# A batched matmul with scale and add on one core: one load per piece of x, another order of transfers, eight shared semaphores, and sixteen tiny loads

## The chip, the core and the metric

The kernel runs on one core of a Trainium2 chip. A core has five engines that run their own instruction lists beside each other: TensorE (PE, matmul), VectorE (DVE), ScalarE (ACT), GpSimd (POOL) and SyncE (SP), which here issues the DMA transfers. Sixteen DMA engines move the data between the chip's memory (HBM) and the core's own memory (SBUF); the matmul writes its sums to PSUM. Engines wait for each other by semaphores. The metric is the time of one execution on the device in microseconds (us). Before the change it is 209.91 us, the median of three runs that lie between 209.87 and 209.99.

## The reference

```python
batch, m, k, n = 16, 512, 1024, 768        # all float32; scale = 0.1
out = scale * np.matmul(x, weight) + add_value
```

x is 16 x 512 x 1024, weight 1024 x 768 and shared by the batch, add_value and the output 16 x 512 x 768. Flattened, it is one matmul of 8192 x 1024 by 1024 x 768 with an element-wise end. Reading x, add_value and weight and writing the output makes 87 MB.

## The kernel before

**Tiles.** The 8192 rows are 64 tiles of 128 rows (`T`). The row that partition p holds in tile t is chosen so that consecutive tiles of one partition lie next to each other in HBM: a transfer of 8 tiles is, for each of 128 partitions, one contiguous piece (32 KB of x, 24 KB of add_value or output). A tile of one tensor is called a slot here. In SBUF there are 16 slots for x (`xs`), used as a ring, and 32 slots for add_value (`ao`), also a ring; the result overwrites add_value in its slot, and the output is written from there. The weights arrive as float32 in slots 16 to 23 of `ao` before add_value needs these.

**The stream.** The string `STREAM` sets the order of all transfers: `x16+8` is x, tiles 16 to 23, `a` is add_value, `o` the output, `w` the weights. SyncE goes through it in order (`sync_engine`), on one queue. Before each transfer it waits for what that transfer needs: an x piece for the casts that empty its slots of the ring (`by_act`, `by_pool`), an add_value piece for the landing of the output that used its slots before (`carriers`), an output for the VectorE work on its tiles (`made`). A transfer behind a waiting one waits too. Each of the 27 transfers in the block has a semaphore of its own that tells of its landing (`landed`). The last one, `o60+4`, is issued behind the block, when all engines are through.

**Moves.** For four tiles at a time (`mover`, 16 moves) ScalarE and GpSimd cast x to bf16, eight casts each, on 32 partitions at a time and regrouped by quarters, into one of two buffers `va`. They start a move when its x has landed and the buffer is free.

**Turns.** VectorE transposes two tiles at a time in blocks of 32 x 32 (`turn`), on pairs of bf16 values taken as one float32, into one half of `xt`; with the regrouping in the moves this is the transpose of the whole 128 x 128 piece.

**Matmuls.** TensorE loops over groups of four tiles (`tensor_engine`). For each tile there are eight pieces of x of 128 x 128 (`KJ`), and each is multiplied with 768 columns of the weights in two matmuls, of 512 and of 256 columns (`CUT`), since a PSUM bank holds 512 float32 of a partition. `xt[q, j // 2]` is the stationary operand, loaded into the array by a weight load (PEld, LDWEIGHTS) that goes with every matmul.

**Finish.** VectorE multiplies the sums of two tiles by the scale and adds add_value, in one instruction (`finish`), and signals `made`. It then transposes the pair after next.

Of the kernel before, what the change touches and what calls it, by code (L numbers as in the profile page):

```python
# [7 lines left out]
P = 128  # L8
G = 16
X_SLOTS = 16  # L10
A_SLOTS = 32
W_SLOT = 16
CUT = 512
MM_BUFS = 4
XT_TILES = 4
VA_BUFS = 2
MOVE = 4

STREAM = """
    x0+4 w0+4 w4+4 x4+8 a0+8 a8+8 x12+4 x16+8 a16+16 x24+8 o0+8 x32+8 o8+8 a32+8 x40+8  # L20
    a40+8 x48+8 o16+8 o24+8 a48+4 x56+8 a52+4 a56+8 o32+16 o48+4 o52+8 o60+4
"""


def transfers():
    for word in STREAM.split():
        s, n = word[1:].split("+")
        yield word[0], int(s), int(n)
# [3 lines left out]
def kernel(  # L32
# [8 lines left out]
    nc = tc.nc  # L41
    bf16 = mybir.dt.bfloat16
    fp32 = mybir.dt.float32
# [5 lines left out]
    _, N = weight.shape  # L49
    T = M // P  # L50
    MOVES = T // MOVE
    KC = K // (2 * P)
    KJ = 2 * KC
# [6 lines left out]
    def rows(view, s, n):  # L60
        assert s // G == (s + n - 1) // G
        return view[:, s // G, s % G:s % G + n, :]

    const = ctx.enter_context(tc.tile_pool(name="const", bufs=1))
# [4 lines left out]
    w_bf = const.tile([P, KJ, N], bf16, name="w_bf")  # L69
    va = [const.tile([P, MOVE * KC, 4, 64], bf16, name=f"va{i}") for i in range(VA_BUFS)]  # L70
    xt = const.tile([P, XT_TILES, KC, P], fp32, name="xt")
    mm = psum.tile([P, MM_BUFS, 1024], fp32, name="mm")

    stream = list(transfers())
    landed = [tc.alloc_semaphore(f"{op}{s}") for op, s, n in stream[:-1]]
    by_act, by_pool, pool_go, turned, casts, done, made = (
        tc.alloc_semaphore(name)
        for name in ("by_act", "by_pool", "pool_go", "turned", "casts", "done", "made"))
    TURNED = MOVE * VA_BUFS
    MADE = TURNED + MM_BUFS  # L80

    def carriers(op, s, n):
        return [sem for (o, a, k), sem in zip(stream, landed)
                if o == op and a < s + n and s < a + k]

    def slots(op, s, n):
        ring = X_SLOTS if op == "x" else A_SLOTS
        k = s % ring
        assert k + n <= ring
        return slice(k, k + n)  # L90

    def engine(eng):
        known = {}

        def need(sem, value):
            if known.get(sem.num if hasattr(sem, "num") else id(sem), 0) < value:
                eng.wait_ge(sem, value)  # L97
                known[sem.num if hasattr(sem, "num") else id(sem)] = value

        return need  # L100

    def transfer(eng, op, s, n):
        if op == "w":
            dst = ao[:, W_SLOT + s:W_SLOT + s + n, :].rearrange("p (c r) n -> p c (r n)", r=2)
            return eng.dma_start(dst, w_v[:, s // 2:(s + n) // 2, :])  # L105
        if op == "x":
            return eng.dma_start(xs[:, slots(op, s, n), :], rows(x_v, s, n))  # L107
        if op == "a":
            return eng.dma_start(ao[:, slots(op, s, n), :], rows(add_v, s, n))  # L109
        return eng.dma_start(rows(out_v, s, n), ao[:, slots(op, s, n), :])  # L110

    def sync_engine(eng):
        need = engine(eng)
        for (op, s, n), sem in zip(stream, landed):
            last = s + n
            if op == "x" and last > X_SLOTS:
                moved = 8 * -(-(last - X_SLOTS) // MOVE)
                need(by_act, moved)
                need(by_pool, moved)
            if op == "a":  # L120
                if s < W_SLOT + KJ <= A_SLOTS and last > W_SLOT:
                    need(casts, KJ)
                if s >= A_SLOTS:
                    for old in carriers("o", s - A_SLOTS, n):
                        need(old, 16)
            if op == "o":
                need(made, MADE + last)
            transfer(eng, op, s, n).then_inc(sem, 16)

    def mover(eng, copy, parity, count, go=None):  # L130
        need = engine(eng)
        if go is None:
            eng.preload_act_table(mybir.ActivationFunctionType.Copy)  # L133
        for q in range(MOVES):
            for sem in carriers("x", MOVE * q, MOVE):
                need(sem, 16)
            if q >= VA_BUFS:
                need(turned, TURNED + MOVE * (q - VA_BUFS + 1))
            if go is not None:
                eng.sem_inc(go, 1)  # L140
            k = MOVE * q % X_SLOTS
            src = xs[:, k:k + MOVE, :].rearrange("p i (c b k) -> p (i c) b k", b=4, k=64)
            for a in (parity, parity + 2):
                for b in range(4):
                    copy(va[q % VA_BUFS][32 * b:32 * b + 32, :, a, :],  # L145
                         src[32 * a:32 * a + 32, :, b, :]).then_inc(count, 1)

    def vector_engine(eng):
        need = engine(eng)

        def cast_w(s, n):
            for sem in carriers("w", s, n):
                need(sem, 16)
            eng.tensor_copy(w_bf[:, s:s + n, :], ao[:, W_SLOT + s:W_SLOT + s + n, :]).then_inc(casts, n)  # L154

        def turn(pair):
            move, half = divmod(pair, 2)
            need(by_act, 8 * (move + 1))
            need(by_pool, 8 * (move + 1))
            if pair > 1:  # L160
                need(done, 4 * (pair - 1))
            q = 2 * half * KC
            eng.transpose(  # L163
                xt[:, 2 * half:2 * half + 2, :, :].rearrange("p i c m -> p (i c m)"),
                va[move % VA_BUFS][:, q:q + 2 * KC, :, :].bitcast(fp32).rearrange("p c a k -> p (c a k)"),
            ).then_inc(turned, 2)

        def finish(pair):
            for sem in carriers("a", 2 * pair, 2):
                need(sem, 16)  # L170
            need(done, 4 * (pair + 1))
            a = ao[:, slots("a", 2 * pair, 2), :]
            q = 2 * (pair % 2)
            eng.scalar_tensor_tensor(  # L174
                a, mm[:, q:q + 2, 0:N], float(scale), a,
                op0=mybir.AluOpType.mult, op1=mybir.AluOpType.add).then_inc(made, 2)

        for op, s, n in stream:
            if op == "w":
                cast_w(s, n)  # L180
        turn(0)
        turn(1)
        for pair in range(T // 2):
            finish(pair)
            if pair + 2 < T // 2:
                turn(pair + 2)

    def tensor_engine(eng):
        eng.sem_inc(turned, TURNED)
        eng.sem_inc(made, MADE)  # L190
        eng.wait_ge(casts, KJ)
        with eng.Fori(TURNED + 2, TURNED + 2 + T, XT_TILES) as i:
            for q in range(XT_TILES):
                if q % 2 == 0:
                    eng.wait_ge(turned, i + q if q else i)
                    eng.wait_ge(made, i + q if q else i)
                for j in range(KJ):
                    x2 = xt[:, q, j // 2, :].bitcast(bf16).rearrange("p (m r) -> p r m", r=2)
                    for n0, n1 in ((0, CUT), (CUT, N)):
                        m = eng.matmul(  # L200
                            mm[:, q, n0:n1], x2[:, j % 2, :], w_bf[:, j, n0:n1],
                            start=(j == 0), stop=(j == KJ - 1))
                if q % 2:
                    m.then_inc(done, 4)

    with tc.tile_critical(no_gpsimd_drain=True):  # L206
        sync_engine(nc.sync)
        mover(nc.scalar, nc.scalar.copy, 0, by_act)
        mover(nc.gpsimd, nc.gpsimd.tensor_copy, 1, by_pool, pool_go)
        vector_engine(nc.vector)  # L210
        tensor_engine(nc.tensor)
# [36 lines left out]
```

## Time and profile before

| | us |
|---|---|
| median of three runs | 209.91 |
| the profiled execution's own time | 210.03 |
| its span, first to last instruction | 208.3 |
| PE busy, matmuls | 171.8 |
| PEld busy, weight loads beside the matmuls | 101.4 |
| DVE busy | 97.7 |
| ACT busy | 134.7 |
| POOL busy | 135.7 |
| DMA queue, share of 16 engines over the span | 97.9% |
| HBM read, written | 61.87 MB, 25.17 MB |

The profile shows one execution. Busy times are shares of the span; an engine that is busy is not for that reason what the others wait for. The page's slices cut the span into 40 equal parts and show, in tenths, how busy each engine and the DMA engines are in each. The chain of waits is followed back from the last instruction to what released it, and so on. In the rows of instructions, L200 is line 200 of the kernel, an "SPq" row is the issue of a transfer on SyncE, and "A <-B" says that A's idle time ended when B was done. A transfer lands some time after it is issued, since the transfers issued before it on the queue go first. The granted clock of TensorE is 0.983 of full speed over the span.

### The profile page before, as it was taken

Reading aid. Unit: us, or ns where it says so; the run is one execution under the profiler, and the core shown is the slowest. Engines: PE = TensorE matmul, PEld = TensorE weight load, DVE = VectorE, ACT = ScalarE, POOL = GpSimd, SP = SyncE. Lnnn points to the kernel's source line nnn. Section 1 sums busy time; section 2 is a strip of 40 time slices with the busy share of each in tenths; the row PEclk is TensorE's granted clock in tenths of the full one; section 3 lists DMA queues with packets and bytes.
Section 4 is the critical chain, followed back from the end, with each engine's and each line's share of the span. In section 5 each row is a group of like instructions: output and inputs, shape, how many; then the busy total and the mean of one; then the engine's idle time right before and its main releaser. Section 6 shows DMA issues by size and latency. Waiting matters only on the chain.

```text
span 208.3 us, 2633 instructions
## 1 busy us (share of the span) xinstructions
PE 171.8 (82%) x1024; PEld 101.4 (49%) x1024; DVE 97.7 (47%) x66; ACT 134.7 (65%) x129; POOL 135.7 (65%) x132
## 2 busy tenths in 40 slices
PE   0000997999999999889999999999999993999930
PEld 0000454666666666546666666566666661566610
DVE  0045206455555555375555553755555533455330
ACT  2492199959799707999997079999980099920000
POOL 0397099959799807999999069999990099930000
PEclk9999999999999999999999999999999999699996
DMA  6999999999999999999999999999999999998975
GB/s 230 408 470 403 453 439 397 426 494 409 403 453 453 403 404 444 458 409 403 430 434 441 419 439 452 415 420 430 439 430 441 403 448 458 434 453 366 446 335 231
DMA packets 4147, 87.06 MB, mean 418 GB/s; under 512 B 432, under 2 KB 432, under 8 KB 944
## 3 DMA queue, kind: packets, MB, share of 16 engines
q1 hardware_dynamic: 4144, 87.03, 97.9%
q14 instruction: 3, 0.02, 0.0%
HBM read 61.87 MB, written 25.17 MB: 418 GB/s over the span
## 4 chain that ended last, share of the span: by engine, by line
DMA 53%; POOL 16%; ACT 11%; PE 11%; issue 2%; DVE 1%; SPq 1%; POOLq 0%; DVEq 0%
DMA xs<-in_x_dram 53%; POOL va L145 16%; ACT va L145 11%; PE mm L200 11%; DVE ao L174 1%; DVE xt L163 1%; SPq L109 0%; SPq L107 0%; SPq L105 0%; POOLq L140 0%; DVEq L97 0%; SPq L97 0%; SPq L243 0%; SPq L206 0%
## 5 line engine op out<-in xcount | busy, mean ns | idle before, releaser
L200 PE MATMUL mm<-w_bf,xt 128*128 128x512 bf16 (+1 forms) x1024 | 171.8, 332 | 27.6 <-DVE xt L163 27.6
L145 POOL CAST va<-xs 32x1024 bf16<-32x1024 f32 x128 | 135.5, 1059 | 48.1 <-DMA xs<-in_x_dram 40.9
L145 ACT CAST va<-xs 32x1024 bf16<-32x1024 f32 x128 | 133.5, 1043 | 47.9 <-DMA xs<-in_x_dram 44.8
L200 PEld LDWEIGHTS mm<-w_bf,xt 128*128 128x128 bf16 x1024 | 101.4, 99 | 97.7 <-DVE xt L163 29.1
L174 DVE SCALAR_TENSOR_TENSOR ao<-mm,ao 128x1536 f32<-128x1536 f32 x32 | 56.1, 1754 | 77.4 <-PE mm L200 62.6
L163 DVE STREAM_TRANSPOSE xt<-va 128x1024 f32<-128x1024 f32 x32 | 39.5, 1235 | 12.5 <-POOL va L145 12.5
L154 DVE CAST w_bf<-ao 128x3072 bf16<-128x3072 f32 x2 | 4.2, 2116 | 13.6 <-DMA ao<-in_weight_dram 13.6
L133 ACT ACT_TABLE_LOAD x1 | 1.3, 1283 | 0.9 <-SPq L206 0.9
L229 POOL MEMSET const-float32-0.0<- 128x1 f32 x1 | 0.1, 98 | 0.2 <-issue 0.2
L229 POOL MEMSET const-bfloat16-1.0<- 128x1 bf16 x1 | 0.1, 101 | 0.0
L229 POOL MEMSET const-float32-1.0<- 128x1 f32 x1 | 0.1, 98 | 0.0
L229 POOL MEMSET const-uint8-127<- 128x1 uint8 x1 | 0.1, 98 | 0.0
## 6 DMA issues: line engine op xcount, KB each, us to landing
xs<-in_x_dram SPq DMA_DIRECT2D x7, 4096.0 KB, 23.7
ao<-in_add_value_dram SPq DMA_DIRECT2D x5, 3072.0 KB, 24.7
out_dram<-ao SPq DMA_DIRECT2D x5, 3072.0 KB, 31.3
ao<-in_add_value_dram SPq DMA_DIRECT2D x1, 6144.0 KB, 34.4
out_dram<-ao SPq DMA_DIRECT2D x1, 6144.0 KB, 38.1
xs<-in_x_dram SPq DMA_DIRECT2D x2, 2048.0 KB, 24.1
ao<-in_weight_dram SPq DMA_DIRECT2D x2, 1536.0 KB, 12.2
ao<-in_add_value_dram SPq DMA_DIRECT2D x2, 1536.0 KB, 17.3
```

The lines of the kernel that those rows point to most:

```text
L133: eng.preload_act_table(mybir.ActivationFunctionType.Copy)
L145: copy(va[q % VA_BUFS][32 * b:32 * b + 32, :, a, :], src[32 * a:32 * a + 32, :, b, :]).then_inc(count, 1)
L154: eng.tensor_copy(w_bf[:, s:s + n, :], ao[:, W_SLOT + s:W_SLOT + s + n, :]).then_inc(casts, n)
L163: eng.transpose(xt[:, 2 * half:2 * half + 2, :, :].rearrange("p i c m -> p (i c m)"), va[move % VA_BUFS][:, q:q + 2 * KC, :, :].bitcast(fp ...
L174: eng.scalar_tensor_tensor(a, mm[:, q:q + 2, 0:N], float(scale), a, op0=mybir.AluOpType.mult, op1=mybir.AluOpType.add).then_inc(made, 2)
L200: m = eng.matmul(mm[:, q, n0:n1], x2[:, j % 2, :], w_bf[:, j, n0:n1], start=(j == 0), stop=(j == KJ - 1))
L229: nc = _bacc.Bacc("TRN2", target_bir_lowering=False, num_devices=1)
```

## The change

Four things change.

- TensorE: the second matmul of each piece (256 columns) is written as a bare instruction without a weight load of its own, and uses the piece that the first one loaded. 512 weight loads are left of 1024.
- The stream has another order from `o0` on, and other sizes. There are still 27 transfers, and the bytes are the same.
- The 27 landing semaphores become eight, shared in turn: transfer i uses lane i mod 8, and its landing is told by a count that goes up by 16. Before it issues transfer i, SyncE waits until transfer i-8 has landed.
- Sixteen tiny loads are added, `narrow`: k rows of the weights for k from 1 to 8, eight loads from SyncE's queue (16 to 128 bytes a row) and eight from ScalarE's (208 to 320 bytes a row), into a tile `spare` that nothing reads. SyncE issues its eight between x12+4 and x16+8, ScalarE its eight behind its table load and ahead of its first cast. SyncE waits for all of them before the first output.

```diff
 STREAM = """
-    x0+4 w0+4 w4+4 x4+8 a0+8 a8+8 x12+4 x16+8 a16+16 x24+8 o0+8 x32+8 o8+8 a32+8 x40+8
-    a40+8 x48+8 o16+8 o24+8 a48+4 x56+8 a52+4 a56+8 o32+16 o48+4 o52+8 o60+4
+    x0+4 w0+4 w4+4 x4+8 a0+8 a8+8 x12+4 x16+8 a16+16 x24+8 o0+16 x32+4 x36+8 a32+8 x44+4
+    a40+8 o16+8 x48+4 x52+8 a48+8 o24+8 x60+4 a56+8 o32+16 o48+4 o52+8 o60+4
 """
...
+    spare = const.tile([P, 2, PROBES, 96], fp32, name="spare")
...
-    landed = [tc.alloc_semaphore(f"{op}{s}") for op, s, n in stream[:-1]]
+    lanes = [tc.alloc_semaphore(f"lane{i}") for i in range(LANES)]
+    landed = [(lanes[i % LANES], 16 * (i // LANES + 1)) for i in range(len(stream) - 1)]
...
+    def narrow(eng, side, sem):
+        for k in range(1, PROBES + 1):
+            n = 4 * k + 48 * side
+            eng.dma_start(spare[0:k, side, k - 1, 0:n], weight[0:k, 0:n]).then_inc(sem, 16)
...
     def sync_engine(eng):
         need = engine(eng)
-        for (op, s, n), sem in zip(stream, landed):
+        for (op, s, n), (sem, mark) in zip(stream, landed):
             last = s + n
+            if mark > 16:
+                need(sem, mark - 16)
+            if (op, s) == ("x", X_SLOTS):
+                narrow(eng, 0, narrow_sp)
...
             if op == "o":
+                need(narrow_sp, 16 * PROBES)
+                need(narrow_act, 16 * PROBES)
                 need(made, MADE + last)
...
         if go is None:
             eng.preload_act_table(mybir.ActivationFunctionType.Copy)
+            narrow(eng, 1, narrow_act)
...
+    def matmul_again(eng, product, piece, weights, start, stop):
+        return eng.add_instruction(mybir.InstMatmult(
+            name=nc.get_next_instruction_name(),
+            engine=eng.engine,
+            ins=[eng.lower_ap(weights), eng.lower_ap(piece)],
+            outs=[eng.lower_ap(product)],
+            start_tensor_calc=start,
+            stop_tensor_calc=stop,
+            tile_size=(P, P),
+            tile_position=(0, 0),
+            ldweights=False,
+        ))
...
-                    for n0, n1 in ((0, CUT), (CUT, N)):
-                        m = eng.matmul(
-                            mm[:, q, n0:n1], x2[:, j % 2, :], w_bf[:, j, n0:n1],
-                            start=(j == 0), stop=(j == KJ - 1))
+                    piece = x2[:, j % 2, :]
+                    flags = dict(start=(j == 0), stop=(j == KJ - 1))
+                    eng.matmul(mm[:, q, 0:CUT], piece, w_bf[:, j, 0:CUT], **flags)
+                    m = matmul_again(eng, mm[:, q, CUT:N], piece, w_bf[:, j, CUT:N], **flags)
```

More of the change, by code (lines that the diff above doesn't have):

```diff
@@ L17 @@
 MOVE = 4
+LANES = 8
+PROBES = 8
 STREAM = """
-    x0+4 w0+4 w4+4 x4+8 a0+8 a8+8 x12+4 x16+8 a16+16 x24+8 o0+8 x32+8 o8+8 a32+8 x40+8
-    a40+8 x48+8 o16+8 o24+8 a48+4 x56+8 a52+4 a56+8 o32+16 o48+4 o52+8 o60+4
+    x0+4 w0+4 w4+4 x4+8 a0+8 a8+8 x12+4 x16+8 a16+16 x24+8 o0+16 x32+4 x36+8 a32+8 x44+4
+    a40+8 o16+8 x48+4 x52+8 a48+8 o24+8 x60+4 a56+8 o32+16 o48+4 o52+8 o60+4
 """
@@ L78 @@
         for name in ("by_act", "by_pool", "pool_go", "turned", "casts", "done", "made"))
+    narrow_sp, narrow_act = tc.alloc_semaphore("narrow_sp"), tc.alloc_semaphore("narrow_act")
     TURNED = MOVE * VA_BUFS
@@ L82, in carriers @@
     def carriers(op, s, n):
-        return [sem for (o, a, k), sem in zip(stream, landed)
+        return [mark for (o, a, k), mark in zip(stream, landed)
                 if o == op and a < s + n and s < a + k]
@@ L95, in need @@
         def need(sem, value):
-            if known.get(sem.num if hasattr(sem, "num") else id(sem), 0) < value:
+            if known.get(id(sem), 0) < value:
                 eng.wait_ge(sem, value)
-                known[sem.num if hasattr(sem, "num") else id(sem)] = value
+                known[id(sem)] = value
         return need
@@ L124, in sync_engine @@
                     for old in carriers("o", s - A_SLOTS, n):
-                        need(old, 16)
+                        need(*old)
             if op == "o":
+                need(narrow_sp, 16 * PROBES)
+                need(narrow_act, 16 * PROBES)
                 need(made, MADE + last)
@@ L133, in mover @@
             eng.preload_act_table(mybir.ActivationFunctionType.Copy)
+            narrow(eng, 1, narrow_act)
         for q in range(MOVES):
-            for sem in carriers("x", MOVE * q, MOVE):
-                need(sem, 16)
+            for mark in carriers("x", MOVE * q, MOVE):
+                need(*mark)
             if q >= VA_BUFS:
@@ L151, in cast_w @@
         def cast_w(s, n):
-            for sem in carriers("w", s, n):
-                need(sem, 16)
+            for mark in carriers("w", s, n):
+                need(*mark)
             eng.tensor_copy(w_bf[:, s:s + n, :], ao[:, W_SLOT + s:W_SLOT + s + n, :]).then_inc(casts, n)
@@ L168, in finish @@
         def finish(pair):
-            for sem in carriers("a", 2 * pair, 2):
-                need(sem, 16)
+            for mark in carriers("a", 2 * pair, 2):
+                need(*mark)
             need(done, 4 * (pair + 1))
```

## The prediction

> **What bounds the kernel now.** I read the page first: engine shares, the slices, the queue's share.
>
> ```profile
> span 208.3 us, 2633 instructions
> PE 171.8 (82%) x1024; PEld 101.4 (49%) x1024; DVE 97.7 (47%) x66; ACT 134.7 (65%) x129; POOL 135.7 (65%) x132
> DMA  6999999999999999999999999999999999998975
> q1 hardware_dynamic: 4144, 87.03, 97.9%
> ```
>
> No compute engine is full, but the one DMA queue is: packets fill 97.9% of 16 engines over the span, 203.9 us, and 87.03 MB in that time is 427 GB/s. Only 4.4 us is not DMA work. The table by stretches shows where (a packet is booked where it starts, so a share may pass 1):
>
> ```profile
> core 0: us, PE busy (x) PEld busy (x) DVE busy (x) ACT busy (x) POOL busy (x), PEclk, DMA share, GB/s
> 0.00:1.90 1.90, 0.00 (x0) 0.00 (x0) 0.00 (x0) 1.00 (x1) 0.20 (x4) 1.00 0.00 0
> 1.90:2.90 1.00, 0.00 (x0) 0.00 (x0) 0.00 (x0) 0.28 (x1) 0.00 (x0) 1.00 1.20 262
> 2.90:70.00 67.10, 47.62 (x275) 27.78 (x276) 29.75 (x20) 48.33 (x47) 50.38 (x46) 1.00 1.01 434
> 70.00:120.00 50.00, 48.43 (x299) 28.93 (x297) 26.45 (x19) 35.08 (x34) 35.40 (x35) 1.00 0.99 423
> 160.00:176.00 16.00, 13.25 (x82) 7.82 (x80) 5.89 (x5) 9.35 (x9) 8.90 (x9) 1.00 1.01 435
> 192.00:201.00 9.00, 7.42 (x46) 4.31 (x44) 3.27 (x3) 0.00 (x0) 0.00 (x0) 1.00 1.01 433
> 201.00:201.50 0.50, 0.00 (x0) 0.00 (x0) 0.28 (x1) 0.00 (x0) 0.00 (x0) 1.00 0.24 98
> 201.50:202.00 0.50, 0.00 (x0) 0.00 (x0) 0.00 (x0) 0.00 (x0) 0.00 (x0) 1.00 0.00 0
> 202.00:202.50 0.50, 0.00 (x0) 0.00 (x0) 0.00 (x0) 0.00 (x0) 0.00 (x0) 1.00 0.76 319
> ```
>
> Apart from 1.9 us before the first packet, the queue has one hole, at 201 to 202.5, where the shares sum to 1.00 x 0.5 us: about 1.0 us is lost. The chain, the instructions in order of time and the last issue's group tell why:
>
> ```profile
> 4.07 40.88 DMA xs<-in_x_dram
> 53.92 25.29 DMA xs<-in_x_dram
> 145.94 20.49 DMA xs<-in_x_dram
> 176.76 22.67 PE mm L200 x128
> 199.53 1.76 DVE ao L174
> 201.57 0.33 SPq L110 DMA_DIRECT2D out_dram<-ao  x1
> out_dram<-ao SPq DMA_DIRECT2D x1, 1536.0 KB, 5.7
> ```
>
> The last x pieces (x56+8) land at 166.43; the last eight tiles leave TensorE at 199.43, VectorE at 201.29; o60+4 is issued at 201.57 and lands 5.7 us later, at 207.26. The chain shown before that is a chain of loads: compute waits for the queue. Does the hole set the end? The queue's window from 206.2 to 206.9 says no:
>
> ```profile
> DMA packets 10, 0.01 MB, mean 18 GB/s; under 512 B 9, under 2 KB 9, under 8 KB 9
> q1 hardware_dynamic: 10, 0.01, 4.8%
> ```
>
> Nine packets are semaphore writes, one a row of data, and 4.8% of 16 x 0.7 us is 0.54 engine-us: one DMA engine still moves its last row while the others sign off. I read it as a straggler that had o52+8 left to do while the other fifteen stood in the hole, and so lost nothing to it. Closing the hole then frees engines that do not end the run.
>
> **The change part by part.** *New stream order.* The bytes are the same, and 27 transfers still go through the queue ahead of o60+4's end. At 427 GB/s an x slot (0.524 MB) is 1.228 us, an a or o slot (0.393 MB) 0.921 us. I start from the landing of x12+4 at 44.95 (4.07 + 40.88), up to which the order is unchanged. x16+8 54.8, a16+16 69.5, x24+8 79.3 (the trace has 53.92 + 25.29 = 79.21, so the rate holds), then o0+16 94.1, x32+4 99.0, x36+8 108.8, a32+8 116.2, x44+4 121.1, a40+8 128.5, o16+8 135.8, x48+4 140.7, x52+8 150.6, a48+8 157.9, o24+8 165.3, x60+4 170.2, a56+8 177.6, o32+16 192.3, o48+4 196.0, o52+8 203.4, o60+4 207.0, against 207.26 in the trace. It holds only if each transfer is issued before the queue runs dry, so I check what each issue waits for, with these rows:
>
> ```profile
> L145 POOL CAST va<-xs 32x1024 bf16<-32x1024 f32 x128 | 135.5, 1059 | 48.1 <-DMA xs<-in_x_dram 40.9
> L174 DVE SCALAR_TENSOR_TENSOR ao<-mm,ao 128x1536 f32<-128x1536 f32 x32 | 56.1, 1754 | 77.4 <-PE mm L200 62.6
> L163 DVE STREAM_TRANSPOSE xt<-va 128x1024 f32<-128x1024 f32 x32 | 39.5, 1235 | 12.5 <-POOL va L145 12.5
> L200 PEld LDWEIGHTS mm<-w_bf,xt 128*128 128x128 bf16 x1024 | 101.4, 99 | 97.7 <-DVE xt L163 29.1
> 67.29 1.76 DVE L174 SCALAR_TENSOR_TENSOR ao<-mm,ao 128x1536 f32<-128x1536 f32 x1 [2.29 <-PE mm L200]
> 166.62 17.49 POOL L145 CAST va<-xs 32x1024 bf16<-32x1024 f32 x16 [10.26 <-DMA xs<-in_x_dram]
> 149.68 23.56 PE L200 MATMUL mm<-w_bf,xt 128*128 128x512 bf16 x144
> ```
>
> A move of four tiles is 8 casts on each of POOL and ScalarE, with gaps 17.49/2 = 8.75 us; a matmul is 23.56/144 = 164 ns, so a tile (16) 2.6 us and a pair 5.2. o0+16 waits for 16 tiles: the eighth pair's VectorE add ends at 67.29 + 1.76 = 69.1; the queue has x24+8 until 79.3, 10 us of cover. Behind it in SP wait x32+4 (ready earlier) and x36+8 (moves 0 to 6, 79.3 + 8.75 = 88; cover until 99). a32+8 needs o0+16 landed, 94.1 against 108.8. x48+4 needs x32+4 moved: 107.8 against 135.8. x52+8 needs x36+8 moved, 108.8 + 2 x 8.75 = 126.3 against 140.7. a48+8: 135.8 against 150.6. x60+4 needs move 11, 135, and is behind a48+8 in SP: 136 against 165.3. The tightest is a56+8, which needs o24+8 landed: 165.3 against x60+4's end at 170.2, less 0.9 us from issue to first packet (201.57 to about 202.4): 4 us of cover. Each microsecond by which o24+8 lands later than that costs one.
>
> The tail: moves 13 and 14 (x52+8, landed 150.6) end at 159.4 and 168.1, the move of x60+4 (170.2) at 179. TensorE takes tiles 52 to 55 at 160.6 to 171, 56 to 59 until 181.5, 60 to 63 until 192; with the add o60+4 is ready near 194, not 201.6, and the queue is busy with o52+8 until 203.4. The hole goes (its 1.0 us), but by the straggler the gain on the end is between 0 and 1.0 us; I take 0, as the sign-off row is the nearest.
>
> *Pieces loaded once.* 512 of 1024 LDWEIGHTS go. Each is 99 ns beside matmuls that average 164, so the saving on TensorE is between 0 and 512 x 0.099 = 50 us, and I take 0, the pace being set by the matmuls. On the end it is 0 in either case, as TensorE leaves the path: the cover is 194 to 203, so TensorE could be 7 us slower, too.
>
> *Eight shared semaphores.* Before transfer i SP now waits for transfer i-8. The most that are queued ahead in my schedule is five (at 97 us: x32+4, x36+8, a32+8, x44+4, a40+8), so i-8 has always landed: 0. A wait that is met already delays only SP, behind the same covers.
>
> *Sixteen tiny loads.* Their issues first:
>
> ```profile
> 4.07 30.68 SPq L107 DMA_DIRECT2D xs<-in_x_dram  x2
> 0.90 1.28 ACT L133 ACT_TABLE_LOAD   x1 [0.90 <-SPq L206]
> 8.19 2.11 ACT L145 CAST va<-xs 32x1024 bf16<-32x1024 f32 x2 [6.00 <-DMA xs<-in_x_dram]
> L109 SPq DMA_DIRECT2D ao<-in_add_value_dram x8: 328/386/877, 3.0 to 153.0; - x8
> ```
>
> An issue is 0.33 to 0.88 us, so eight take 2.6 to 7.0. On SP they stand after x12+4 at 4.5, and end by 11.5 at worst, where SP waits for x16+8's casts until 34 anyway. On ScalarE they start after the table load, at 2.2, and end between 4.8 and 9.2; the first cast starts at 8.19, so at most 1.0 us late, which x16+8 has 10 us to absorb (issued at 34.4, queue full to 44.95). Then the engines' time. The last semaphore write, in a window of 0.05 us around 206.78:
>
> ```profile
> DMA packets 1, 0.00 MB, mean 0 GB/s; under 512 B 1, under 2 KB 1, under 8 KB 1
> q1 hardware_dynamic: 1, 0.00, 1.1%
> ```
>
> 1.1% of 16 x 0.05 us is 9 ns. If every tiny load puts a data and a semaphore packet of that size on one engine, it is 16 x 18 = 0.29 us. At the other end each read stands alone: the first microsecond of the queue moved 262 instead of 434 GB/s, 0.4 us lost from cold, so 8 x 0.4 = 3.2 us a queue and 6.4 for both in turn. I take 0.2, since 432 semaphore writes already run through a queue whose share is 1.01. On fourteen or fifteen engines that falls into slack (1.0 of hole and 0.5 of sign-off, 1.5 us); on the straggler it counts. On the end: 0.1.
>
> The Trainium skill speaks against this part. In "DMA: Bandwidth & Descriptors", "Why a DMA increments its semaphore by 16 and not by 1", a load of k rows from SP or ACT runs on the k lowest-numbered engines, so the low ones would get nearly all of it; no row here numbers an engine. [...]
>
> Sum: 210.03 (the profiled execution's own time, 208.3 of span and 1.7 around it) + 0 + 0 + 0 + 0.1, less the 0.12 by which that execution lies over the median of 209.91: 210.0.
>
> **Rivals.** *A, tiny loads hold an engine (slower).* From cold, one after another, 3.2 us on an engine that takes part in all of a queue's eight, 1.5 absorbed: 211.7. It decides from 1.5 us, 94 ns a load. For: the 262 GB/s row. Against: the 9 ns packet, and that other work is queued behind them.
>
> *B, the straggler is not an engine but an order of reads and writes (faster).* Then all engines end at the mean, 1.9 + 203.9 = 205.8, in place of the last sign-off at 206.8: 209.0; if the slow 423 GB/s stretch goes as well, (434 - 423)/434 x 50 = 1.3 us more, 207.7. For: fifteen engines do wait in the hole. Against: one engine late at the very end with the hole behind it.
>
> *C, a56+8 late (slower).* If o24+8, a write, lands 6 us late, 2 us of hole, 212. Against: the 4 us of cover.
>
> *D, the compiler still loads twice.* 1024 LDWEIGHTS remain; 210.0 as well, as TensorE is covered.
>
> **How the numbers follow.** This kernel's three runs lie within 0.12 us, so 0.2% (0.42 us) is what I call a change. Main case, D in it, 0.45, its own range 209.5 to 210.4; it gives same 0.41, and 0.02 to either side. B 0.25, all faster; A 0.22 and C 0.08, all slower. So faster 0.27, same 0.41, slower 0.32. The range leaves out B's far end and the upper parts of A and C: 208.6 to 211.8.
>
> **What would show it.** Queue share near 1.00 from 2.9 us to the end with no hole at 201; o60+4 issued near 194 and landing more than 10 us later; LDWEIGHTS x512; x60+4 landing near 170; SP's longest waits ended by casts and writes, none by an old transfer; one engine still last at the sign-off. Wrong if the first transfers after the tiny loads (x16+8) land over 1 us later than the schedule's 54.8, if a hole opens before a56+8, or if the engines end together.

## The result: 0.37% slower

The changed kernel takes 210.76 us, the median of 18 runs (210.05 to 212.62), beside 210.09 us for the kernel before in the same rounds (18 runs, 209.78 to 210.89). The ratio is 1.0037, with a 95% interval of 1.0024 to 1.0050. It was measured again on another occasion, beside its own version without the tiny loads (run r1 below), and came out the same: 1.0037 (1.0024 to 1.0050).

The profiled execution of the first measurement happens to be the slowest of the 18 (212.62 us, a span of 210.8). For what is typical I read the profile of r1, the same kernel, whose profiled execution took 210.73 us. The head of its page:

```profile
span 208.9 us, 2135 instructions
PE 170.4 (82%) x1008; PEld 50.8 (24%) x512; DVE 97.9 (47%) x66; ACT 134.7 (64%) x129; POOL 135.4 (65%) x132
DMA  6999999999999999999999999999999999998994
```

The weight loads (PEld) are halved, from 1024 to 512, and TensorE is as busy as before (171.8 us then; a few matmul records are missing now). The DMA line still is the full one. The instructions of the first profile in order of time show when the tiny loads are issued (SyncE's and ScalarE's issues; start, duration, count):

```profile
4.56 4.25 SPq L120 DMA_DIRECT2D spare<-in_weight_dram  x8
0.93 3.27 ACTq L120 DMA_DIRECT2D spare<-in_weight_dram  x8
8.56 1.04 ACT L162 CAST va<-xs 32x1024 bf16<-32x1024 f32 x1 [6.37 <-DMA xs<-in_x_dram]
```

SyncE's issues end at 8.81, within the prediction's 11.5, and ScalarE's at 4.20, a little ahead of its 4.8, since they go out while its table load runs. Nothing waits for them so early. The first cast starts at 8.56 instead of 8.19, when its x has landed.

The difference is in the queue. The table by stretches of r1, first the middle and then the end; the last two columns are the share and GB/s of the DMA engines:

```profile
166.00:180.00 14.00, 13.95 (x88) 4.20 (x43) 8.72 (x6) 11.01 (x11) 11.38 (x11) 1.00 1.03 418
180.00:192.00 12.00, 11.95 (x76) 3.62 (x37) 5.82 (x4) 0.00 (x0) 0.00 (x0) 1.00 0.97 418
...
203.00:205.00 2.00, 0.00 (x0) 0.00 (x0) 0.00 (x0) 0.00 (x0) 0.00 (x0) 0.50 1.01 430
205.00:205.50 0.50, 0.00 (x0) 0.00 (x0) 0.00 (x0) 0.00 (x0) 0.00 (x0) 0.50 0.81 344
205.50:206.00 0.50, 0.00 (x0) 0.00 (x0) 0.00 (x0) 0.00 (x0) 0.00 (x0) 0.50 0.64 270
206.00:206.50 0.50, 0.00 (x0) 0.00 (x0) 0.00 (x0) 0.00 (x0) 0.00 (x0) 0.50 0.35 147
206.50:207.00 0.50, 0.00 (x0) 0.00 (x0) 0.00 (x0) 0.00 (x0) 0.00 (x0) 0.50 0.12 49
207.00:207.50 0.50, 0.00 (x0) 0.00 (x0) 0.00 (x0) 0.00 (x0) 0.00 (x0) 0.50 0.12 49
```

The hole at 201 to 202.5 of the kernel before is gone, as forecast: TensorE is through in time, and the queue has work until the end. But the DMA engines do not stop together. From 205 on one after another falls idle, and from 206.5 two of sixteen (0.12) are left. The run ends when the last one does. The same rows of the changed kernel without its tiny loads (run r2) end a microsecond sooner:

```profile
166.00:180.00 14.00, 13.95 (x87) 4.20 (x43) 7.61 (x6) 9.70 (x10) 10.17 (x10) 1.00 1.07 456
180.00:192.00 12.00, 11.89 (x74) 3.62 (x37) 5.79 (x4) 0.00 (x0) 0.00 (x0) 1.00 0.92 396
...
204.00:204.50 0.50, 0.00 (x0) 0.00 (x0) 0.00 (x0) 0.00 (x0) 0.00 (x0) 0.50 1.03 442
204.50:205.00 0.50, 0.00 (x0) 0.00 (x0) 0.00 (x0) 0.00 (x0) 0.00 (x0) 0.50 0.64 270
205.00:205.50 0.50, 0.00 (x0) 0.00 (x0) 0.00 (x0) 0.00 (x0) 0.00 (x0) 0.50 0.12 49
205.50:206.00 0.50, 0.00 (x0) 0.00 (x0) 0.00 (x0) 0.00 (x0) 0.00 (x0) 0.50 0.12 49
206.00:206.50 0.50, 0.00 (x0) 0.00 (x0) 0.00 (x0) 0.00 (x0) 0.00 (x0) 0.50 0.06 25
```

### The profile page after: what moved, and what is told of

Read it like the earlier page. It is cut to its first block, busy times and chain, and to the rows that moved or that the text cites. A ratio compares the mean times of both kernels' runs of the same rounds, so it can differ in the third digit from the quotient of the medians.

```text
span 210.8 us, 2135 instructions
## 1 busy us (share of the span) xinstructions
PE 167.7 (80%) x1008; PEld 50.4 (24%) x512; DVE 98.2 (47%) x66; ACT 134.7 (64%) x129; POOL 135.6 (64%) x132
## 4 chain that ended last, share of the span: by engine, by line
PE 49%; DMA 32%; POOL 8%; DVE 1%; SPq 1%; issue 1%; POOLq 0%; DVEq 0%
DMA xs<-in_x_dram 32%; PE mm L231 32%; PE mm L206 17%; POOL va L162 8%; DVE ao L191 1%; DVE xt L180 1%; SPq L112 0%; SPq L114 0%; SPq L110 0%; POOLq L157 0%; DVEq L102 0%; SPq L273 0%; SPq L102 0%; SPq L236 0%
## 5 line engine op out<-in xcount | busy, mean ns | idle before, releaser
L231 PE MATMUL mm<-w_bf,xt 128*128 128x512 bf16 x496 | 163.8, 382 | 27.2 <-DVE xt L180 27.2
L206 PE MATMUL mm<-w_bf,xt 128*128 128x256 bf16 x512 | 140.3, 274 | 0.8
L231 PEld LDWEIGHTS mm<-w_bf,xt 128*128 128x128 bf16 x512 | 50.4, 98 | 144.9 <-issue 116.4
L171 DVE CAST w_bf<-ao 128x3072 bf16<-128x3072 f32 x2 | 4.7, 2326 | 13.6 <-DMA ao<-in_weight_dram 13.6
```

What stands on the lines that cost most here:

```text
L206: return eng.add_instruction(mybir.InstMatmult(name=nc.get_next_instruction_name(), engine=eng.engine, ins=[eng.lower_ap(weights), eng.low ...
L231: eng.matmul(mm[:, q, 0:CUT], piece, w_bf[:, j, 0:CUT], **flags)
```

## The experiments

Every kernel was timed in five rounds beside the kernel before. The edits show the lines that matter; where tiny loads are added or left out, their definition or the waits for them are, too. The ratios are to the kernel before, with their 95% intervals.

```
run                  edit                                              median us  ratio (95%)
e1_tiny_alone        before + the sixteen tiny loads                   210.65     1.0024 (1.0012 to 1.0035)
e2_order_alone       before + the new order                            210.10     0.9992 (0.9982 to 1.0003)
e9_weights_alone     before + one weight load a piece                  209.61     0.9980 (0.9970 to 0.9991)
e3, r2               changed - tiny loads (two measurements)           209.74     0.9983 (0.9972 to 0.9993), 0.9983 (0.9973 to 0.9994)
e4_old_order         changed, old order                                210.61     1.0024 (1.0011 to 1.0036)
r1_changed_again     changed                                           210.89     1.0037 (1.0024 to 1.0050)
e5_sp_only           changed, SyncE's tiny loads only                  210.06     1.0007 (0.9991 to 1.0023)
e6_act_only          changed, ScalarE's tiny loads only                209.91     0.9993 (0.9981 to 1.0005)
e7_sp_later          changed, SyncE's only, ahead of a32+8             209.90     0.9994 (0.9981 to 1.0008)
e8_sp_16rows         changed, SyncE's only, 16 rows each               210.46     1.0019 (1.0005 to 1.0033)
e10_32_one_row       changed, 32 of one row from SyncE, none of ACT    215.27     1.0249 (1.0233 to 1.0264)
```

A second table is worked out from the semaphore updates in the traces, one trace of each kernel. Each transfer over 128 partitions is signed off by sixteen DMA engines, and the traces do not say which sign-off is which engine's. "At" is when the last of the sixteen signs, "spread" how long that is after the first.

```
                     x12+4          x16+8          x24+8          o52+8           o60+4
                     at     spread  at     spread  at     spread  at      spread  at
before               44.95  0.43    54.66  0.44    79.21  0.53    203.61  2.37    207.26
r2 (no tiny)         45.08  0.55    54.79  0.54    79.19  0.50    203.35  1.97    207.00
e6 (ACT's only)      45.02  0.51    54.73  0.49    79.33  0.61    203.14  1.78    206.78
e7 (SP's, later)     44.96  0.38    54.68  0.39    79.44  0.73    203.63  2.37    207.27
e5 (SP's only)       45.00  0.51    55.03  0.80    80.76  2.09    204.16  2.39    207.81
r1 (changed)         45.03  0.44    55.46  1.13    81.18  2.33    204.39  2.32    208.02
e1 (tiny alone)      45.06  0.51    55.34  1.08    81.21  2.45    204.32  3.09    207.95
e8 (16 rows)         45.09  0.51    55.65  0.63    80.44  1.17    204.19  2.25    207.83
e10 (32 of one row)  44.93  0.37    59.66  5.38    84.51  5.80    208.93  3.31    212.59
```

### Which of the parts costs the time

e1, the kernel before with the tiny loads alone:

```diff
+            if (op, s) == ("x", X_SLOTS):
+                narrow(eng, 0, narrow_sp)
...
             eng.preload_act_table(mybir.ActivationFunctionType.Copy)
+            narrow(eng, 1, narrow_act)
```

> The kernel before with the sixteen tiny loads alone. The changed kernel was 0.37% slower (0.24 to 0.50%). If the tiny loads cost it, by the time they take on the low-numbered DMA engines, this kernel is slower by as much, 0.3 to 0.4%. If the order of the transfers costs it, by which loads meet slow stretches of the memory, this one is within 0.1% of before. By the prediction's own term (0.1 us) it is 0.05% slower.

e2, the kernel before with the string `STREAM` of the changed one:

```diff
-    x0+4 w0+4 w4+4 x4+8 a0+8 a8+8 x12+4 x16+8 a16+16 x24+8 o0+8 x32+8 o8+8 a32+8 x40+8
+    x0+4 w0+4 w4+4 x4+8 a0+8 a8+8 x12+4 x16+8 a16+16 x24+8 o0+16 x32+4 x36+8 a32+8 x44+4
...
```

> The kernel before with the new order of the stream alone. If the order costs the 0.37%, this one is 0.3 to 0.4% slower, with stretches in which DMA moves under 400 GB/s that the kernel before does not have. If the tiny loads do, it is within 0.1% of before, or faster by up to 0.5% if the hole before the last transfer counted.

e3, the changed kernel without the tiny loads (`spare` is left empty):

```diff
-            if (op, s) == ("x", X_SLOTS):
-                narrow(eng, 0, narrow_sp)
...
-            narrow(eng, 1, narrow_act)
```

> The changed kernel without the sixteen tiny loads. If the tiny loads cost the 0.37%, it is within 0.1% of before; if the order does, it stays 0.3 to 0.4% slower; if the single weight load or the shared semaphores do, it also stays slower while the kernel with the order alone does not.

e4, the changed kernel with the `STREAM` of before:

```diff
-    x0+4 w0+4 w4+4 x4+8 a0+8 a8+8 x12+4 x16+8 a16+16 x24+8 o0+16 x32+4 x36+8 a32+8 x44+4
+    x0+4 w0+4 w4+4 x4+8 a0+8 a8+8 x12+4 x16+8 a16+16 x24+8 o0+8 x32+8 o8+8 a32+8 x40+8
...
```

> The changed kernel with the old order of the stream. If the order costs the 0.37%, it is within 0.1% of before; if the tiny loads do, it stays 0.3 to 0.4% slower.

The four agree that the tiny loads cost the time. With them it is 0.24% over before (e1 and e4), without them it is not over before at all (e2, e3). Against e3 they cost the changed kernel 1.0037/0.9983, which is 0.54%, or 1.1 us. In the kernel before they cost 0.24% (e1); each ratio is known to about 0.1%, so part of this difference can be noise. The order by itself is worth nothing that can be measured: e2 has no hole before o60+4, and its last transfer lands at 207.32, against 207.26 before. This is the prediction's reading of the hole.

### Whether it repeats

The expectations from here on speak of "theory lag": the tiny loads make one or a few DMA engines late, an engine that is late stays late, and the run ends with the latest one.

> The changed kernel once more, beside its own version without tiny loads on the same chip. Theory lag: 0.2 to 0.5% slower than before, and landings of x24+8 spread by more than 2 us. If the first measurement was an accident of the chip it ran on, it is within 0.1% of before.

> The changed kernel without tiny loads once more, on the same chip. Theory lag: 0.1 to 0.3% faster than before, and 0.4 to 0.6% faster than the changed kernel. If the gain was an accident, within 0.1% of before.

Both ratios came out within 0.01% of the first measurement. It was no accident of one occasion. The version without tiny loads is faster than both kernels, by 0.17% and 0.54%.

### Which queue, which place, how many rows

e5 leaves out ScalarE's eight, e6 SyncE's eight:

```diff
 # e5
-            narrow(eng, 1, narrow_act)
 # e6
-            if (op, s) == ("x", X_SLOTS):
-                narrow(eng, 0, narrow_sp)
```

> The changed kernel without ScalarE's eight tiny loads; SyncE's eight stay between x12+4 and x16+8. Theory lag: SyncE's loads make one or a few DMA engines late at 45 us, by some 0.6 us, the late engine loses more in the slow reads of x24+8 at 77 us, and as it ends behind all others, the run is longer. Then this kernel is as slow as the changed one, 0.3 to 0.4% over before. Rival queue: the second queue (ScalarE's) is what costs, since every DMA engine then serves two rings; then this one is 0.1 to 0.2% faster than before, like the kernel without tiny loads.

> The changed kernel without SyncE's eight tiny loads; ScalarE's eight stay. Theory lag: their lag is at the start (landing of x0+4 spread by 0.55 to 0.74 us instead of 0.41 to 0.48) and is gone by w0+4, so 0.1 to 0.2% faster than before. Rival queue: 0.3 to 0.4% slower than before.

In time the two are not separated (1.0007 and 0.9993, intervals that overlap). In the traces they are. Without SyncE's loads (e6) nothing falls behind: x16+8 and x24+8 land as in r2. With them (e5) x16+8 spreads to 0.80 and x24+8 to 2.09 us, and the last transfer lands 0.8 us later than in r2. So the lag that the traces show comes from SyncE's loads. The time does not confirm that they cost all of it. e5's median is lower than the lag theory forecast, 0.24% over r2, where all sixteen loads cost 0.54%, and its profiled execution (210.52 us) is slower than its median (210.06). Whether ScalarE's loads add something when both sets are there is open.

e7 moves SyncE's eight behind x36+8:

```diff
-            narrow(eng, 1, narrow_act)
...
-            if (op, s) == ("x", X_SLOTS):
+            if (op, s) == ("a", A_SLOTS):
                 narrow(eng, 0, narrow_sp)
...
-                need(narrow_sp, 16 * PROBES)
+                if s >= 16:
+                    need(narrow_sp, 16 * PROBES)
```

> The changed kernel with SyncE's eight tiny loads alone, moved ahead of a32+8, so that they run at some 109 us, behind the slow reads at 77 us. Theory lag with the second loss at 77 us: only the first 0.6 us is left, no jump to 2.4 us at x24+8, and the late engine stays ahead of the one that is slow in writes (2.2 us at the end): 0 to 0.2% faster than before. Rival, the cost is the same wherever the loads stand: 0.3 to 0.4% slower than before.

The chain of waits shows the load that differs. In the changed kernel (r1) x24+8 lands 27.19 us after its issue at 53.99:

```profile
53.99 27.19 DMA xs<-in_x_dram
```

and in e7, whose tiny loads come later, 25.50 us after 53.94, close to the 25.29 of the kernel before:

```profile
53.94 25.50 DMA xs<-in_x_dram
```

In e7 the spread grows from 0.81 us at x36+8 to 1.50 at a32+8, right behind the tiny loads. That is little more than it grows there without any (0.70 to 1.31 in e2, 0.74 to 1.14 in r2), and o60+4 lands at 207.27, as before the change, with a spread of 2.37 us that e2 has too (2.38). So in the traces the place matters: these eight loads leave no lag that can be told from that of kernels without them. The times do not settle it: e7 (0.9994) is on the side of the theory, but its interval and e5's overlap.

e8 gives each of the eight loads 16 rows:

```diff
-            eng.dma_start(spare[0:k, side, k - 1, 0:n], weight[0:k, 0:n]).then_inc(sem, 16)
+            eng.dma_start(spare[0:16, side, k - 1, 0:n], weight[0:16, 0:n]).then_inc(sem, 16)
```

> The changed kernel with SyncE's eight tiny loads alone, in the old place, each of 16 rows instead of 1 to 8, so that every DMA engine gets eight rows. Theory lag by uneven loads: all engines are late by the same, up to 0.6 us, none falls behind the others at 45 us (spread under 0.6 us at x16+8), and the time is from 0.2% faster than before to 0.2% slower. Rival, a cost for each tiny load whatever its rows: as slow as the changed kernel, 0.3 to 0.4% over before, or more.

Here the eight loads have 128 sign-offs, sixteen each, so every engine carries all eight. x16+8 lands at 55.65 instead of 54.79 with hardly any more spread (0.63 against 0.54): all engines are about 0.86 us late, 0.11 us for each load. The kernel is 0.19% slower than before, within the theory's range and under the 0.3% of the rival; the lag is even, as the theory said, but larger than its 0.6 us.

e10 puts 32 loads of one row in the old place:

```diff
-PROBES = 8
+PROBES = 32
...
-            eng.dma_start(spare[0:k, side, k - 1, 0:n], weight[0:k, 0:n]).then_inc(sem, 16)
+            eng.dma_start(spare[0:1, 0, k - 1, 0:16], weight[0:1, 16 * k:16 * k + 16]).then_inc(sem, 16)
```

> The changed kernel with 32 tiny loads of one row of 64 bytes from SyncE in the old place, and none from ScalarE, so that all of them run on one DMA engine. The loads of 16 rows made every engine some 0.9 us later for eight, 0.11 us each. Theory lag: one engine falls 3 to 4 us behind at x16+8 and keeps that to the end; less the 2.2 us by which an engine slow in writes ends late anyway, the run ends 1.3 us later than without tiny loads, and 1.3 more if it loses again at x24+8: 0.4 to 1.1% slower than before. Rival, no lasting lag (other packets fill the time): within 0.2% of before.

One engine falls 4.87 us behind at x16+8 (59.66 against 54.79), 0.15 us for each load, and does not catch up: the spread is still 5.46 us at o24+8. The tiny loads' own packets do not take that time. They start one behind the other between 44.36 and 44.82, 14 ns for each load. The time is in the packet of x16+8 that starts right behind them. Two windows of e10's DMA queue show it: in the first (44.82 to 44.83) that packet alone starts, in the second (45.2 to 45.7) fifteen others do:

```profile
DMA packets 1, 0.03 MB, mean 3277 GB/s; under 512 B 0, under 2 KB 0, under 8 KB 0
q1 hardware_dynamic: 1, 0.03, 3361.9%
DMA packets 15, 0.49 MB, mean 983 GB/s; under 512 B 0, under 2 KB 0, under 8 KB 0
q1 hardware_dynamic: 15, 0.49, 228.3%
```

A packet's whole time is booked where it starts. So the first 32 KB took 33.619 x 16 x 0.01 = 5.38 us, while each of the fifteen took 2.283 x 16 x 0.5 / 15 = 1.22 us. The issues on SyncE, and two stretches of the queue, late in e10:

```profile
4.50 34.82 SPq L119 DMA_DIRECT2D spare<-in_weight_dram  x32
39.45 1.07 SPq L112 DMA_DIRECT2D xs<-in_x_dram  x1
```

```profile
168.00:170.50 2.50, 2.50 (x17) 0.69 (x8) 0.92 (x1) 2.45 (x3) 2.32 (x4) 1.00 0.13 56
...
210.00:211.00 1.00, 0.00 (x0) 0.00 (x0) 0.00 (x0) 0.00 (x0) 0.00 (x0) 0.50 0.06 25
211.00:212.00 1.00, 0.00 (x0) 0.00 (x0) 0.00 (x0) 0.00 (x0) 0.00 (x0) 0.50 0.06 25
```

At the end one engine of sixteen (0.06) works alone for two microseconds. And at 168 to 170.5 the other fifteen have next to nothing to do (share 0.13): a56+8 waits for all sixteen to have written o24+8, so the one late engine holds back the issue, and that time, 2.2 us, is lost by all. By their first sign-offs the fast engines end x60+4 at the same time as in r2 (168.51 and 168.53) and a56+8 4.1 us later (180.10 and 176.00), so the queue is slow behind the hole, too. This is why the run is 2.5% longer, and not the 0.4 to 1.1% that I expected from the lag alone.

### The single weight load

e9, the kernel before with the part of the change that concerns TensorE (`matmul_again` is defined as in the change):

```diff
-                    for n0, n1 in ((0, CUT), (CUT, N)):
-                        m = eng.matmul(
-                            mm[:, q, n0:n1], x2[:, j % 2, :], w_bf[:, j, n0:n1],
-                            start=(j == 0), stop=(j == KJ - 1))
+                    piece = x2[:, j % 2, :]
+                    flags = dict(start=(j == 0), stop=(j == KJ - 1))
+                    eng.matmul(mm[:, q, 0:CUT], piece, w_bf[:, j, 0:CUT], **flags)
+                    m = matmul_again(eng, mm[:, q, CUT:N], piece, w_bf[:, j, CUT:N], **flags)
```

> The kernel before with the single weight load of each piece alone. TensorE is covered by the queue in the prediction: within 0.1% of before, with 512 weight loads and the same pace of some 163 ns a matmul. Rival: the weight loads held TensorE up, and with them gone the last tiles are done earlier and the hole before o60+4 shrinks: 0.1 to 0.5% faster.

The kernel before with this alone is 0.20% faster (0.09 to 0.30%). VectorE's last two adds, in order of time in e9:

```profile
194.00 1.76 DVE L174 SCALAR_TENSOR_TENSOR ao<-mm,ao 128x1536 f32<-128x1536 f32 x1 [2.29 <-PE mm L189]
199.20 1.76 DVE L174 SCALAR_TENSOR_TENSOR ao<-mm,ao 128x1536 f32<-128x1536 f32 x1 [3.44 <-PE mm L189]
```

A pair of tiles takes 199.20 - 194.00 = 5.20 us on TensorE, the same pace as the 5.2 us that I had worked out for the kernel before. The whole tail is 0.33 us earlier than before (199.53), because x56+8 lands at 166.13 instead of 166.43. So the gain is not in TensorE's pace. Nor is it a matter of the granted clock: among executions at 0.98 or more alone, e9's median is 209.59 (7 runs) and that of the kernel before 209.98 (14 runs), still 0.19%. The queue is a little faster, and why it is with half the weight loads is not settled; one trace of each kernel cannot tell 0.3 us from the differences between runs. The shared semaphores were not tried alone. With the order and the single loads beside them the ratio is 0.9983, with the single loads alone 0.9980, so they leave no sign that can be seen at about 0.1%.

## Why the prediction was right, and where it was wrong

The range (208.6 to 211.8) holds the time, and the bound was named rightly. The likeliest case, no change within 0.2%, did not come; the outcome of rival A, slower because tiny loads hold an engine, did, with less than half of its 1.7 us (0.7 us over the kernel before). That the range holds the time is owed to the rivals: the sum itself gave 210.0, with 0.1 us for the part that cost 1.1.

- **What bounds the kernel.** Right. The changed kernel's queue has work from the first packet to the last, and each kernel that ended later did so by its DMA engines.
- **The hole before o60+4 is worth nothing.** Right for the profiled executions, and e2, which closes it, stays at 0.9992 (0.9982 to 1.0003). But this is an average. In e2's rounds the kernel before has a median of 209.9 in its 20 executions with a granted clock of 0.98 or more and of 210.47 in its 10 below 0.9735, where e2 has 210.11 (5 executions). A later TensorE makes the hole longer, so at the lower clock it may be worth the difference of 0.36 us; no trace of such an execution of the kernel before was kept, and this is not shown.
- **The schedule of the new order.** The landings are right within a microsecond where the tiny loads do not disturb them. I had a56+8 wait for o24+8 until 165.3 and x60+4 land at 170.2; in r2 these are 165.04 and 169.92. o60+4 is issued at 195.83 in r2, forecast near 194. In the changed kernel itself (r1) it is issued at 199.5 and lands 8.5 us later, not the more than 10 that I named as a sign: TensorE waited for the late x24+8 until 91.5 (89.4 in r2) and then had a granted clock of 0.50 for 3.4 us, which r2's does not have there. The queue was busy with o52+8 until 204.39, so the cover of 7 us was needed in part and held.
- **Single weight loads: 0.** Right for TensorE's pace, wrong by a little for the end: 0.2% was gained, and the cause is open.
- **Shared semaphores: 0.** No run contradicts it. (The block issues 26 of the 27 transfers, so there were 26 such semaphores; o60+4 is issued behind it.)
- **Sixteen tiny loads: 0.2 us on an engine, 0.1 on the end.** This is the step that failed. I took 18 ns for a load, from the 9 ns of a semaphore packet, since many such packets run through a full queue. The packets of the tiny loads are that short in the trace, too, but the data packet behind them is longer (5.38 instead of 1.22 us in e10). The runs show 0.11 us (e8) to 0.15 us (e10) of an engine's time for each load from SyncE. The price is not constant: the eight loads of 1 to 8 rows make x16+8 land 0.67 us later than in r2 in r1, but only 0.24 in e5, which is 0.08 and 0.03 us a load. All are under rival A's 0.4 us. Its threshold of 94 ns was 1.5 us over sixteen loads; ScalarE's eight left no lag (e6), and at x16+8 the other eight came to less than 1.5 us.
- **The slack of 1.5 us.** It was too large. x24+8 makes the late end later still: the spread goes from 1.13 to 2.33 us there in r1, and from 0.54 to 0.50 without the loads (r2). Since the traces do not number the engines, that it is the same engine each time is inferred. I had no term for a late engine that becomes later.
- **"Wrong if x16+8 lands over 1 us later."** It landed 0.2 to 0.8 us later in r1, e1 and e5 than in r2 and before. The mark was set too far out.

Where the 1.0 us between r1 and r2 goes can be read from the rows above. 0.36 us is spread: the last engine ends 2.32 instead of 1.96 us behind the first (o60+4). The rest is common to all engines. From 166 to 192 they moved 14 x 418 + 12 x 418 = 10,868 KB in r1 and 14 x 456 + 12 x 396 = 11,136 KB in r2; the 268 KB less are 0.63 us at 427 GB/s, at a share that was about full in both. The first sign-offs say the same: they are 0.14 us later than in r2 for x60+4, 0.58 for a56+8 and 0.66 for o60+4. So it is a56+8 whose reading took longer. This slow reading of a56+8 is in all three traces that have the new order and SyncE's tiny loads of 1 to 8 rows at 45 us (393 GB/s in the changed kernel's first profile from 166 to 180, 418 in e5 and r1) and not in e7 (449), in e8, where all engines are late alike (446), nor in e1 with the old order (451). Why a late engine makes the reads of the others slower is open.

The Trainium skill has, in "DMA: Bandwidth & Descriptors", "Why a DMA increments its semaphore by 16 and not by 1", that a load of k rows (k up to 16) from SyncE or ScalarE runs on k engines, the lowest-numbered. The traces agree as far as they can: 32 loads of one row made one engine late by 4.87 us, eight loads of 16 rows made all late by about the same 0.86 us. They do not show which engines these are. This was the right warning, and I gave it too little weight.

## What to carry to other kernels

When the DMA queue is full from end to end, the run ends with its latest DMA engine, so look at the spread of the sign-offs and not only at the share. In such a queue a tiny load cost the engines that carried it far more than its packets last, 0.03 to 0.15 us here, and a lag that arose at 45 us could still be seen at the end (r1, e10). It depends on the place: ScalarE's eight at the start (e6) and SyncE's eight ahead of a32+8 (e7) left no lag that lasted. Each wait for a whole transfer waits for the latest engine, so one late engine can in the end stop all sixteen, as in e10.

## What was unexpected

- A tiny load of 16 to 128 bytes a row takes 0.03 to 0.15 us of an engine although its packets last 9 to 13 ns in the trace. Why the data packet behind it is longer is open.
- The reads of x24+8 near 77 us are slow in all kernels but e8 (394 to 421 GB/s from 70 to 82, where the kernel before has 437 ahead of it and 430 behind; 438 in e8); an engine that comes there 0.2 to 0.7 us late (e5, r1, e1) leaves it 1.2 to 1.4 us later still, while in e10, late by 5 us, it lost only 0.4 more. The cause is open.
- SyncE needed 34.8 us to issue 32 tiny loads where eight took 4.25 us. They stood behind seven large transfers, so the queue seems to take only so many at once, which is an inference; it cost nothing, as x16+8 was issued at 39.45, still ahead of the end of x12+4 at 44.93.
